# Relu fused into VectorE's add out of PSUM, y held unscaled, and a fourth-power range check on w1

## The chip, the cores and the metric

One core of one Trainium2 chip. The metric is the device time of one execution in microseconds (us), as the median of several runs. Each comparison was made on one chip, but not all on the same one. PE is TensorE's matmul, PEld its weight load, DVE VectorE, ACT ScalarE, POOL GpSimd, SP the engine whose queue issues most stores.

## The reference

```python
batch, m, k, h, n = 16, 512, 768, 3072, 768       # x, w1, b1, w2: standard normal, fp32
y = np.maximum(np.matmul(x, w1) + b1, 0)
return np.matmul(y, w2).astype(np.float32)
```

## The kernel before

Both products run in fp16 with a Strassen-like scheme of seven block products p1 to p7, whose sums are built partly in PSUM. So PE goes on accumulating into a bank *after* ACT has copied the intermediate sum out of it: p6 follows the copy of p1, p7 the copy of p6, in the same bank "a". The rows of x are done in 8 blocks, the hidden dimension in 2 halves, which gives 16 iterations (the first product of the first one is done plainly, so 15 x 6 = 90 groups have the code below); the product groups of neighbouring iterations are interleaved on PE.

```python
def first(self, it, t):                       # one group of the first product
    def copy(name, ps, bias):                 # ACT: intermediate sum out of PSUM
        nc.scalar.activation(out=g[name], in_=ps, func=ACTF.Identity, bias=bias, scale=YS)
    def add(slot, ps, s):                     # DVE: PSUM times 1/16 plus the copy
        nc.vector.scalar_tensor_tensor(out=y[:, slot], in0=ps, scalar=YS, in1=g[s],
                                       op0=ALU.mult, op1=ALU.add)
    ...
    def p3():
        mm(g["c"], self.XS4, self.B22, False)
        add(self.A12, g["c"], "s2")
        nc.vector.tensor_scalar(out=y[:, 0:3], in0=y[:, 0:3], scalar1=0.0,
                                scalar2=None, op0=ALU.max)          # the relu of three blocks
    def p4():
        mm(g["a"], self.XA22, self.T4, False)
        nc.scalar.activation(out=y[:, self.A21], in_=g["a"], func=ACTF.Relu, ...)
        self.sums_y(y)                        # DVE: four sums for the second product
```

fp16 can overflow, so the kernel gathers sums of squares of all inputs on ACT, tests them late, and falls back to a general path when they are out of bounds:

```python
def stat_w(self, stat, c, t, w):              # half c, tile t of w1 or w2
    ...
    self.nc.scalar.activation(out=junk, in_=flat[:, 0:4], func=ACTF.Square,
                              accum_out=self.stat[:, i:i + 1])
...
for t in range(TP):                           # when: iteration c*8+1 for w1, c*8+2 for w2
    at = (t // 2, 1 + 3 * (t % 2))            # (output group, block product)
    put("m2", c * NSB + 1, *at, self.stat_w, "w1", c, t, self.w1s)
    put("m2", c * NSB + 2, *at, self.stat_w, "w2", c, t, self.w2s)
```

## Time and profile before

| | before |
|---|---|
| time, median of 3 | 901.82 us |
| span in the profile | 899.9 us |
| PE, DVE, ACT busy | 98%, 67%, 45% |
| from the 71st matmul's start to the last one's | 877.7 us |

A hole below is the time between two matmul starts beyond the usual spacing (216 ns after one of 512 columns, 162 after one of 384). The lines of the page and how they are read are in the prediction.

### The profile page before, as it was taken

To read this page: it belongs to the slowest core of one execution; us is meant where nothing else is said; L and a number is where in the kernel's file an instruction comes from. 1 tells how busy PE (TensorE), PEld (TensorE's weight loads), DVE (VectorE), ACT (ScalarE), POOL (GpSimd) and SP (SyncE) were. 2 spreads that over 40 slices of the span, in tenths; PEclk is the share of its full clock that TensorE was granted. 3 is DMA by queue.
4 is the path that set the end of the run, shared out by engine and by line. 5 is a ranking of instruction groups with operands and counts; after the bars stand their busy time and mean duration, and the time that the engine had idled before them with its cause. 6 is when DMAs were issued, how large, how long until landed. Compare 5 with 4: busy or idle time off the path is not lost. (4 is left out here: it accounts for less than half of the span.)

```text
span 899.9 us, 13094 instructions
## 1 busy us (share of the span) xinstructions
PE 883.6 (98%) x4775; PEld 468.0 (52%) x4775; DVE 601.2 (67%) x1103; ACT 407.5 (45%) x698; POOL 84.0 (9%) x143
## 2 busy tenths in 40 slices
PE   7999999999999999999999999999999999999997
PEld 4455454554545555454554545545455554545544
DVE  2597838658475674837748677685776858667574
ACT  4757685765555546525434055262513315042220
POOL 7200000010000000012001000101001010010100
PEclk9999999999999999999999999999999999999999
DMA  9999999588675945576749434635445364350613
GB/s 203 201 238 191 339 172 284 106 245 172 148 247 110 307 93 194 210 154 136 193 164 388 161 121 179 210 138 176 151 183 176 129 199 184 120 176 36 211 53 125
DMA packets 106472, 162.53 MB, mean 181 GB/s; under 512 B 67852, under 2 KB 81956, under 8 KB 104356
## 3 DMA queue, kind: packets, MB, share of 16 engines
q1 hardware_dynamic: 67696, 114.44, 37.0%
q0 software_dynamic: 38384, 46.41, 26.0%
q8 instruction: 39, 0.64, 0.3%
q10 hardware_dynamic: 324, 0.80, 0.3%
q14 instruction: 29, 0.24, 0.1%
HBM read 95.37 MB, written 76.48 MB: 191 GB/s over the span
## 5 line engine op out<-in xcount | busy, mean ns | idle before, releaser
L440 PEld LDWEIGHTS <-y 128*128 128x128 f16 x2688 | 263.0, 98 | 190.3 <-issue 5.0
L359 PEld LDWEIGHTS <-w1s 128*128 128x128 f16 x1890 | 184.9, 98 | 212.8 <-issue 1.9
L440 PE MATMUL a<-w2s,y 128*128 128x384 f16 x1536 | 276.2, 326 | 4.2 <-DVE o L445 1.9
L359 PE MATMUL a<-x,w1s 128*128 128x512 f16 x1080 | 267.7, 379 | 0.9 <-DVE y L369 0.8
L365 ACT ACTIVATE s<-a,b1y 128x512 f32<-128x512 f32 x180 | 123.8, 688 | 313.2 <-PE a L359 310.7
L359 PE MATMUL c<-x,w1s 128*128 128x512 f16 x540 | 145.9, 379 | 0.1
L440 PE MATMUL c<-w2s,y 128*128 128x384 f16 x768 | 145.7, 326 | 0.0
L445 DVE SCALAR_TENSOR_TENSOR o<-a,s 128x384 f32<-128x384 f32 x64 | 35.6, 556 | 74.7 <-PE a L440 70.8
L315 DVE TENSOR_TENSOR y<-y 128x512 f16<-128x512 f16 x96 | 40.8, 425 | 65.5 <-ACT y L403 52.9
L369 DVE SCALAR_TENSOR_TENSOR y<-a,s 128x512 f16<-128x512 f32 x90 | 61.6, 685 | 30.6 <-ACT s L365 30.6
L403 ACT ACTIVATE y<-a,b1y 128x512 f16<-128x512 f32 x90 | 61.9, 687 | 30.1 <-PE a L359 30.1
L359 PE MATMUL b<-x,w1s 128*128 128x512 f16 x270 | 73.0, 379 | 0.0
L440 PE MATMUL b<-w2s,y 128*128 128x384 f16 x384 | 72.9, 326 | 0.0
L424 POOL DMA_DIRECT2D o<-out_dram x64 | 34.6, 546 | 388.4 <-DMA out_dram<-o 175.9
L317 DVE TENSOR_TENSOR y<-y 128x1024 f16<-128x1024 f16 x96 | 66.4, 692 | 3.3
L365 ACT ACTIVATE s<-c,b1y 128x512 f32<-128x512 f32 x90 | 61.9, 688 | 8.0 <-PE c L359 8.0
L454 ACT ACTIVATE s<-a 128x384 f32<-128x384 f32 x64 | 31.3, 488 | 71.7 <-PE a L440 71.7
L369 DVE SCALAR_TENSOR_TENSOR y<-b,s 128x512 f16<-128x512 f32 x90 | 61.6, 684 | 2.7 <-PE b L359 1.1
L369 DVE SCALAR_TENSOR_TENSOR y<-c,s 128x512 f16<-128x512 f32 x90 | 61.4, 682 | 0.4
L445 DVE SCALAR_TENSOR_TENSOR o<-b,s 128x384 f32<-128x384 f32 x64 | 35.6, 556 | 31.9 <-PE b L440 15.6
L398 DVE TENSOR_SCALAR y<-y 128x1536 f16<-128x1536 f16 x90 | 50.4, 560 | 3.1
L252 ACT ACTIVATE junk<-xn 128x768 f16<-128x768 f16 x60 | 50.5, 842 | 0.3
(67 smaller groups left out, 439.1 us busy)
## 6 DMA issues: line engine op xcount, KB each, us to landing
out_dram<-o SPq DMA_DIRECT2D x127, 384.0 KB, 3.6
o<-out_dram POOLq DMA_DIRECT2D x64, 384.0 KB, 4.1
xd<-x SPq DMA_DIRECT2D x8, 2688.0 KB, 12.0
x<-xd SPq DMA_DIRECT2D x8, 2688.0 KB, 9.7
xn<-in_x_dram POOLq DMA_DIRECT2D x15, 768.0 KB, 10.3
w1s<-in_w_dram POOLq DMA_DIRECT2D x24, 192.0 KB, 6.5
w2d<-w2t SPq DMA_DIRECT2D x6, 672.0 KB, 3.8
w2s<-w2d SPq DMA_DIRECT2D x6, 672.0 KB, 9.7
```

The costliest lines, as they stand in the source:

```text
L252: self.nc.scalar.activation(out=junk[:, 0:2].rearrange("p a n -> p (a n)"), in_=rows, func=ACTF.Square, accum_out=self.stat[:, i:i + 1])
L315: tt(out=y[:, self.S1], in0=y[:, self.A21], in1=y[:, self.A22], op=ALU.add)
L317: tt(out=y[:, self.S3:self.S2 + 1:self.S2 - self.S3], in0=y[:, self.A21:self.S1 + 1], in1=a11, op=ALU.subtract)
L359: nc.tensor.matmul(ps, lhsT=w[:, slot, k, :], rhs=x[:, xslot, k, :], start=(start and k == 0), stop=(k == 2), skip_group_check=True)
L365: nc.scalar.activation(out=g[name], in_=ps, func=ACTF.Identity, bias=bias, scale=YS)
L369: nc.vector.scalar_tensor_tensor(out=y[:, slot], in0=ps, scalar=YS, in1=g[s], op0=ALU.mult, op1=ALU.add)
L398: nc.vector.tensor_scalar(out=y[:, 0:3], in0=y[:, 0:3], scalar1=0.0, scalar2=None, op0=ALU.max)
L403: nc.scalar.activation(out=y[:, self.A21], in_=g["a"], func=ACTF.Relu, bias=bias1, scale=YS)
L424: self.nc.gpsimd.dma_start(out=o[:, half, :], in_=self.rows_of(it, j, half))
L440: nc.tensor.matmul(ps, lhsT=ys[t][:, op, j * P:(j + 1) * P], rhs=ws[t][:, slot, :], start=(start and t == 0), stop=(t == self.TP - 1), ski ...
L445: nc.vector.scalar_tensor_tensor(out=o, in0=ps, scalar=inv, in1=s, op0=ALU.mult, op1=ALU.add)
L454: nc.scalar.activation(out=to, in_=ps, func=ACTF.Copy, scale=inv)
```

## The change

Its intent is to relieve VectorE. An operation that adds two tensors and clamps the sum between two constants makes the separate relu needless. Both of its constants are bounds, so none is left for a scale, and y is no longer held as 1/16 of itself. An unscaled y comes nearer to fp16's limit, which asks for a sharper bound on w1, a sum of fourth powers, and ACT squares the tile twice.

```diff
-X_HI, W1_HI, W2_HI, B_HI = 64.0, 1500.0, 8000.0, 60000.0
+X_HI, W1_HI, W2_HI, B_HI = 34.0, 50.0, 8000.0, 1300.0
 ...
-        self.nc.scalar.activation(out=junk, in_=flat[:, 0:4], func=ACTF.Square,
+        src = flat[:, 0:4]
+        if stat == "w1":
+            self.nc.scalar.activation(out=junk, in_=src, func=ACTF.Square)
+            src = junk
+        self.nc.scalar.activation(out=junk, in_=src, func=ACTF.Square,
                                   accum_out=self.stat[:, i:i + 1])
 ...
-            nc.vector.scalar_tensor_tensor(out=y[:, slot], in0=ps, scalar=YS, in1=g[s],
-                                           op0=ALU.mult, op1=ALU.add)
+            nc.vector._custom_dve(TENSOR_ADD_SAT, out=y[:, slot], in0=ps, in1=g[s], s0=F_MAX,
+                                  s1=0.0)
 ...
-            nc.vector.tensor_scalar(out=y[:, 0:3], in0=y[:, 0:3], scalar1=0.0,
-                                    scalar2=None, op0=ALU.max)
 ...                                           # second product
-            nc.vector.scalar_tensor_tensor(out=o, in0=ps, scalar=inv, in1=s,
-                                           op0=ALU.mult, op1=ALU.add)
+            nc.vector.tensor_tensor(out=o, in0=ps, in1=s, op=ALU.add)
```

Cut: ACT's `scale=YS` and `scale=inv` and the scaling of b1 go, w1's lower bound becomes 2 instead of 8, and the bounds are filled in to the fourth power for w1.

More of the change, by code (lines that the diff above doesn't have):

```diff
@@ L6 @@
 from concourse._compat import with_exitstack
+from concourse.dve_ops import TENSOR_ADD_SAT
 from concourse.masks import make_identity
@@ L18 @@
 P = 128
-YS = 1.0 / 16.0
-X_HI, W1_HI, W2_HI, B_HI = 64.0, 1500.0, 8000.0, 60000.0
-X_LO, W1_LO, W2_LO = 1.0, 8.0, 0.5
+F_MAX = 3.0e38
+X_HI, W1_HI, W2_HI, B_HI = 34.0, 50.0, 8000.0, 1300.0
+X_LO, W1_LO, W2_LO = 1.0, 2.0, 0.5
 def general_path(ctx, tc, xf, w1, b1, w2, of):
@@ L158, in constants @@
         at = 0
-        for width, hi, lo in ((nw, W1_HI, W1_LO), (nw, W2_HI, W2_LO), (nx, X_HI, X_LO),
-                              (nb, B_HI, 0.0)):
-            nc.gpsimd.memset(self.high[:, at:at + width], hi * hi)
-            nc.gpsimd.memset(self.low[:, at:at + width], lo * lo)
+        for width, hi, lo in ((nw, W1_HI ** 4, W1_LO ** 4), (nw, W2_HI ** 2, W2_LO ** 2),
+                              (nx, X_HI ** 2, X_LO ** 2), (nb, B_HI ** 2, 0.0)):
+            nc.gpsimd.memset(self.high[:, at:at + width], hi)
+            nc.gpsimd.memset(self.low[:, at:at + width], lo)
             at += width
@@ L177, in turn_bias @@
         nc.tensor.transpose(ps[:, 0:nb], rows, self.ident[0:nb, 0:nb])
-        nc.vector.tensor_scalar(out=self.b1y, in0=ps[:, 0:nb], scalar1=YS, scalar2=None,
-                                op0=ALU.mult)
+        nc.vector.tensor_copy(out=self.b1y, in_=ps[:, 0:nb])
         nc.scalar.activation(out=self.stat[:, self.nstat - nb:], in_=ps[:, 0:nb],
@@ L333, in step @@
             nc.scalar.activation(out=y[:, slot], in_=ps, func=ACTF.Relu,
-                                 bias=self.bias_of(0, half, t), scale=YS)
+                                 bias=self.bias_of(0, half, t))
         m1, m2 = (self.XA11, self.XA12), (self.XA21, self.XA22)
@@ L364, in copy @@
             g[name] = self.s_tile(name)
-            nc.scalar.activation(out=g[name], in_=ps, func=ACTF.Identity, bias=bias,
-                                 scale=YS)
+            nc.scalar.activation(out=g[name], in_=ps, func=ACTF.Identity, bias=bias)
         def add(slot, ps, s):
-            nc.vector.scalar_tensor_tensor(out=y[:, slot], in0=ps, scalar=YS, in1=g[s],
-                                           op0=ALU.mult, op1=ALU.add)
+            nc.vector._custom_dve(TENSOR_ADD_SAT, out=y[:, slot], in0=ps, in1=g[s], s0=F_MAX,
+                                  s1=0.0)
         def p1():
@@ L403, in p4 @@
             nc.scalar.activation(out=y[:, self.A21], in_=g["a"], func=ACTF.Relu,
-                                 bias=bias1, scale=YS)
+                                 bias=bias1)
             self.sums_y(y)
@@ L435, in second @@
         g = {}
-        inv = 1.0 / YS
         def mm(ps, op, slot, start):
@@ L453, in take @@
             if part is None:
-                nc.scalar.activation(out=to, in_=ps, func=ACTF.Copy, scale=inv)
+                nc.scalar.activation(out=to, in_=ps, func=ACTF.Copy)
             else:
```

## The prediction

Passages that no trace of this case shows are cut from the text below, and the cuts are marked. Its sum came to 901.8 + 4.6 = 906.4 us. The one term that a cut touches is step 3's, where the estimated time of the plain add is gone; it enters the sum as 0. What the trace gives is the time of the scaled adds that are replaced, 685 ns (L369) and 556 ns (L445); that the new operations would take as long was the estimate. The eight banks of rival (b) are the program's own eight PSUM buffers (pools of 3, 2 and 3).

> **What bounds the kernel now.** I read the page first (busy shares and slices), then the groups by shape, then the waits of PE alone, then the order in time of two stretches. In section 1 PE is busy 98%, DVE 67%, ACT 45%; in section 2 PE is at 9 or more in all slices but the first and the last, and ACT is highest early.
>
> ```profile
> PE 883.6 (98%) x4775; PEld 468.0 (52%) x4775; DVE 601.2 (67%) x1103; ACT 407.5 (45%) x698; POOL 84.0 (9%) x143
> ...
> PE   7999999999999999999999999999999999999997
> ...
> ACT  4757685765555546525434055262513315042220
> ```
>
> A busy PE need not be a fast PE, so I checked its pace. In the timeline three 512-column matmuls start in 0.647 us (216 ns each) and six 384-column ones in 0.974 us (162 ns each), though the records read 379 and 326 ns. The program has 1890 + 144 of the first kind and 2688 of the second: 2034 x 0.216 + 2688 x 0.162 = about 876 us. Of the span of 899.9 us that leaves some 24: 9.7 before the first real matmul, about 5.5 after the last one (last add and store), 2 for transposes, and 6 to 7 of holes. The holes that the waits of PE put on DVE:
>
> ```profile
> PE a L440 <- DVE o L445: 1.9, 2, 1.7
> PE a L440 <- DVE w2s L219: 1.4, 1, 1.4
> PE a L440 <- DVE s L445: 0.9, 1, 0.9
> PE a L359 <- DVE y L369: 0.8, 1, 0.8
> ```
>
> They and two of 0.2 to 0.3 us in the start sum to 5.5 us. That is all that a faster VectorE could ever win. These are the groups that the change touches:
>
> ```profile
> L369 DVE SCALAR_TENSOR_TENSOR y<-a,s 128x512 f16<-128x512 f32 x90 | 61.6, 685 | 30.6 <-ACT s L365 30.6
> ...
> L398 DVE TENSOR_SCALAR y<-y 128x1536 f16<-128x1536 f16 x90 | 50.4, 560 | 3.1
> L315 DVE TENSOR_TENSOR y<-y 128x512 f16<-128x512 f16 x96 | 40.8, 425 | 65.5 <-ACT y L403 52.9 <-ACT y L333 12.4
> ...
> L227 ACT ACTIVATE junk<-w1s 128x1536 f16<-128x1536 f16 x12 | 17.8, 1482 | 0.2
> ```
>
> L398 is the separate relu (90 times); L315, which follows it on DVE, spends 52.9 us waiting for ACT's relu of the fourth product. L227 is the range statistic of w1, 12 times.
>
> [...]
>
> **The change part by part.** (1) **Gone: 90 relus** of 0.560 us, 50.4 us of DVE time, 601 to about 551. The order of instructions is otherwise unchanged on every engine but for part 4. What the relu's time is worth is read in the stretch of first products:
>
> ```profile
> 306.67 0.68 DVE L369 SCALAR_TENSOR_TENSOR y<-c,s 128x512 f16<-128x512 f32 x1
> ...
> 307.39 0.56 DVE L398 TENSOR_SCALAR y<-y 128x1536 f16<-128x1536 f16 x1
> 307.94 0.69 ACT L403 ACTIVATE y<-a,b1y 128x512 f16<-128x512 f32 x1
> ...
> 308.66 0.42 DVE L315 TENSOR_TENSOR y<-y 128x512 f16<-128x512 f16 x1 [0.71 <-ACT y L403]
> ```
>
> DVE finishes the relu at 307.95 and then idles 0.71 us until ACT's activation, which follows the last product on PE, is done. Without the relu the same L315 starts at the same time, after an idle time of some 1.2 us. Gain for PE: 0. The two holes in the final group (0.8 and 0.9 us, at 865 and 869) also lie behind an L315 that waited for L403 with DVE idle (0.53 and 0.42 us), so they stay. The 1.4 us hole at 47 us and the 1.7 us hole at 138 us have other DVE work in front. I allow 0.
>
> (2) **270 adds become add-and-clamp** of an estimated 0.685 us: 0. (3) 384 scaled adds in the second product become plain adds, 0.556 us [...]: 0. ACT's scale becomes 1: 0.
>
> (4) **Added: 12 squares on ACT**, since a fourth power needs two passes over w1. Each costs 1.48 us, and the second pass waits for the first's result on the same engine (some 0.04 us, the gap between dependent statistics in the trace): 1.52 us, 18 us of ACT time. Six of them stand near 550 us, where ACT idles 13.5 us right after the group: six times 1.52 is 9.1, hidden. The other six stand between 107 and 131 us, and there ACT has no room:
>
> ```profile
> 113.50:132.40 18.90, 18.90 (x118) 11.35 (x116) 6.25 (x9) 18.47 (x37) 2.10 (x3) 1.00 0.91 166
> ```
>
> In this stretch of 18.9 us (columns: length, then PE, PEld, DVE, ACT, POOL) ACT is busy 18.47. Five squares more, 7.6 us, can only be had by lagging, and PE needs ACT: it may go on accumulating into a bank only after ACT has copied the intermediate sum out of it.
>
> ```profile
> 121.66 1.48 ACT L227 ACTIVATE junk<-w1s 128x1536 f16<-128x1536 f16 x1
> ...
> 123.05 0.19 ACT L227 ACTIVATION_READ_ACCUMULATOR junk<-w1s 128x1 f32 x1
> 123.26 1.48 ACT L227 ACTIVATE junk<-w1s 128x1536 f16<-128x1536 f16 x1
> ...
> 125.58 2.11 PE L440 MATMUL a<-w2s,y 128*128 128x384 f16 x12
> ...
> 125.72 0.47 ACT L454 ACTIVATE s<-a 128x384 f32<-128x384 f32 x1
> ```
>
> Take the copy at 125.72, done at 126.19. It sits behind two statistics. PE's next product in that bank (the second half of the run at 125.58) starts at 126.56, 0.37 us later. Now add the lag. The first square (107.7) meets 1.3 us of ACT idle time and is absorbed.
> - Copy done at 118.02 moves by 2 x 1.52 to 121.06; PE wanted the bank at 119.73: PE loses 1.3.
> - Copy done at 126.19 moves by 4 x 1.52 to 132.3; PE, late by 1.3, wanted it at 127.9: loses 4.4 (5.7 in all).
> - Copy done at 131.78 moves by 5 x 1.52 to 139.4; PE wanted it at 138.8: loses 0.6 (6.3 in all).
>
> (5) **Given back:** just after, PE already loses 2.05 us in the kernel before (0.23 at 135.7 and 1.82 at 136.5), because a VectorE add waited for a store to free its output buffer:
>
> ```profile
> 134.49 0.56 DVE L445 SCALAR_TENSOR_TENSOR o<-b,s 128x384 f32<-128x384 f32 x1 [4.25 <-DMA out_dram<-o]
> ...
> 138.35 1.14 PE L440 MATMUL a<-w2s,y 128*128 128x384 f16 x6 [1.66 <-DVE o L445]
> ```
>
> That store follows a copy of ACT's that ends at 127.4; it moves by 6.1 to 133.5. In the kernel before the store was issued at about 128.6, behind another, and took 5.9 us; with 4.2 (median of this stretch) to 5.9 us it lands at 137.7 to 139.4. From that add to PE's restart it was 3.86 us, so PE restarts at 141.6 to 143.2. PE, late by 6.3, would want it at 136.3 + 6.3 = 142.6. So it restarts at 142.6 to 143.2, against 138.35 before: a net loss of 4.3 to 4.9 us. Sum: 901.8 + 4.6 = **906.4 us**.
>
> **Rivals.** (a) **VectorE's relief reaches PE**: for it, DVE is 86% busy in the first-product stretch (3.87 of 4.50 us) and some PE holes name it; against it, DVE idles in front of L315. At most 5.5 us, 896 us. (b) **ACT's squares are hidden**, by the eight banks or a lead of ACT that I misjudge: about 901.8 us. For it, ACT is 45% busy over the whole; against it, the stretch above. (c) **The add-and-clamp is slower than one add**, and DVE becomes the bound of the first-product stretch. With the relu gone DVE has about 0.56 + 0.5 = 1.1 us to spare in each group of 4.53 us, so three adds may each grow by 0.35 us, to 1.04. [...] Only the custom nature of the operation speaks for it. (d) The delay of ACT reaches later loads (it frees the buffers of x) and opens a second hole: 1 to 4 us more.
>
> **Range and chances.** The mechanism of part 4 gives 4 to 6.3 us; hidden or helped it falls to 901, with (d) it rises to 910. Range 902.5 to 909.5. Faster by over 2% needs 18 us, more than all holes together: 1%. Slower by over 2% needs (c): 5%. Within 2%: 94%.
>
> **What would show it.** In the profile after: DVE near 551 us, ACT near 425; the clamping adds at 0.68 us (over 1.04 refutes part 2); the first sum of y (L315 before) waiting for ACT's relu some 0.56 us longer in each group; PE's waits with a new line on ACT's copy, about 6 us, all between 119 and 140 us, and none near 550; the hole behind the store at 138 us smaller than 2 us. If PE's waits in that stretch do not grow, part 4 is wrong; if PE's old DVE holes shrink elsewhere, part 1 is.

## The result, and the profile after

The changed kernel takes 908.2 us (median of 4 runs, 906.39 to 908.34), the kernel before 901.38 in the same comparison. The ratio is 1.0073, with a 95% interval of 1.0056 to 1.0091. It is a small loss that is clear of the noise.

Section 1 of the page after, its first line:

```profile
PE 885.0 (98%) x4775; PEld 468.7 (52%) x4775; DVE 551.9 (61%) x1013; ACT 425.0 (47%) x710; POOL 83.5 (9%) x143
```

DVE lost 49.3 us of work and ACT gained 17.5; PE's work is the same 4775 matmuls. The groups by shape after (columns: line, engine, operation, operands and count; busy us, mean ns of one; idle time before, with its releasers):

```profile
L319 DVE TENSOR_TENSOR y<-y 128x512 f16<-128x512 f16 x96 | 40.8, 425 | 116.1 <-ACT y L405 103.7 <-ACT y L337 12.4
L373 DVE CUSTOM_DVE_ANT_0 y<-a,s 128x512 f16<-128x512 f32 x90 | 61.7, 685 | 32.2 <-ACT s L369 32.0
...
L231 ACT ACTIVATE junk<-junk 128x1536 f16<-128x1536 f16 x12 | 17.8, 1483 | 0.4
...
L229 ACT ACTIVATE junk<-w1s 128x1536 f16<-128x1536 f16 x12 | 17.8, 1482 | 0.3
```

The add-and-clamp takes 685 ns, as the scaled add did. The first sum of y, now L319, waits for ACT's relu 103.7 us instead of 52.9: 50.8 us more, 0.56 us a group. The 90 relus had taken 50.4 us: their time turned into waiting. The waits of PE after:

```profile
PE a L441 <- ACT s L454: 5.4, 2, 4.2
...
PE a L441 <- DVE w2s L219: 1.4, 1, 1.4
PE a L441 <- DVE s L446: 0.9, 1, 0.9
PE a L363 <- DVE y L373: 0.8, 1, 0.8
```

New is a wait for ACT's copies, twice. Gone from the list are the 1.9 us on DVE's add L445: 1.66 behind the store at 138 us and 0.24 at 193 us. The other three stand as before, although DVE has less to do. The timeline after, at the two new holes (start, duration, what; idle time before in brackets):

```profile
120.69 0.47 ACT L454 ACTIVATE s<-a 128x384 f32<-128x384 f32 x1
...
121.21 1.14 PE L441 MATMUL a<-w2s,y 128*128 128x384 f16 x6 [1.20 <-ACT s L454]
...
131.89 0.47 ACT L454 ACTIVATE s<-a 128x384 f32<-128x384 f32 x1
...
132.41 2.08 PE L441 MATMUL a<-w2s,y 128*128 128x384 f16 x6 [4.21 <-ACT s L454]
...
132.69 0.15 PEld L441 LDWEIGHTS <-y 128*128 128x128 f16 x1 [0.17 <-issue]
...
133.00 0.15 PEld L441 LDWEIGHTS <-y 128*128 128x128 f16 x1 [0.17 <-issue]
133.32 0.15 PEld L441 LDWEIGHTS <-y 128*128 128x128 f16 x1 [0.17 <-issue]
```

Both products start 0.05 us after a copy ends. After the second hole something was not foreseen: the six matmuls take 2.08 us instead of 1.14, and the weight loads come every 0.32 us, not every 0.16. The windows of the same trace (columns as in the prediction; after POOL come the granted PE clock, the DMA share and GB/s), the hole first and then the matmuls behind it:

```profile
128.30:132.41 4.11, 0.00 (x0) 0.00 (x0) 0.00 (x0) 4.05 (x7) 0.00 (x0) 0.90 0.24 96
132.41:135.63 3.22, 3.22 (x13) 1.61 (x12) 1.03 (x2) 3.22 (x8) 1.41 (x2) 0.59 0.36 23
```

ACT works through the whole hole. Then PE's granted clock is 0.59 on average over 3.2 us; the trace's clock record shows half speed for 3.41 us, from 131.62 to 135.03 us, of which the beginning fell into the hole.

### The profile page after: what moved, and what is told of

It is laid out like the page before. It is cut to its first block, busy times and chain, and to the rows that moved or that the text cites. A ratio compares the mean times of both kernels' runs of the same rounds, so it can differ in the third digit from the quotient of the medians.

```text
span 904.8 us, 13016 instructions
## 1 busy us (share of the span) xinstructions
PE 885.0 (98%) x4775; PEld 468.7 (52%) x4775; DVE 551.9 (61%) x1013; ACT 425.0 (47%) x710; POOL 83.5 (9%) x143
## 5 line engine op out<-in xcount | busy, mean ns | idle before, releaser
L369 ACT ACTIVATE s<-a,b1y 128x512 f32<-128x512 f32 x180 | 123.7, 687 | 305.4 <-PE a L363 302.3
L319 DVE TENSOR_TENSOR y<-y 128x512 f16<-128x512 f16 x96 | 40.8, 425 | 116.1 <-ACT y L405 103.7
L446 DVE TENSOR_TENSOR o<-a,s 128x384 f32<-128x384 f32 x64 | 35.6, 556 | 83.4 <-PE a L441 73.3
L373 DVE CUSTOM_DVE_ANT_0 y<-a,s 128x512 f16<-128x512 f32 x90 | 61.7, 685 | 32.2 <-ACT s L369 32.0
L369 ACT ACTIVATE s<-c,b1y 128x512 f32<-128x512 f32 x90 | 61.9, 688 | 8.1 <-PE c L363 8.1
L373 DVE CUSTOM_DVE_ANT_0 y<-b,s 128x512 f16<-128x512 f32 x90 | 61.6, 684 | 3.0 <-PE b L363 1.3
L373 DVE CUSTOM_DVE_ANT_0 y<-c,s 128x512 f16<-128x512 f32 x90 | 61.5, 683 | 0.4
L446 DVE TENSOR_TENSOR o<-b,s 128x384 f32<-128x384 f32 x64 | 35.6, 556 | 26.3 <-PE b L441 15.6
L446 DVE TENSOR_TENSOR s<-a,o 128x384 f32<-128x384 f32 x64 | 35.6, 556 | 19.5 <-PE a L441 19.5
## 6 DMA issues: line engine op xcount, KB each, us to landing
xn<-in_x_dram POOLq DMA_DIRECT2D x15, 768.0 KB, 10.6
```

The costliest lines, as they stand in the source:

```text
L319: tt(out=y[:, self.S1], in0=y[:, self.A21], in1=y[:, self.A22], op=ALU.add)
L373: nc.vector._custom_dve(TENSOR_ADD_SAT, out=y[:, slot], in0=ps, in1=g[s], s0=F_MAX, s1=0.0)
L446: nc.vector.tensor_tensor(out=o, in0=ps, in1=s, op=ALU.add)
```

## The experiments

All traces were also compared matmul by matmul with that of the kernel before. "Loss" below is the growth of the time from the 71st matmul's start to the last one's; it leaves out the head.

| run | what | median us | ratio to before, 95% interval | loss in the trace, us |
|---|---|---|---|---|
| after | the change | 908.2 | 1.0073 (1.0056 to 1.0091) | +4.8 |
| after_again | the change, second trace | 907.38 | 1.0057 (1.0038 to 1.0076) | +5.1 |
| a1 | a2 with wrong bounds: general path, void | 2912.43 | 3.2298 (3.2234 to 3.2363) | - |
| b1 | before + second squares | 907.35 | 1.006 (1.004 to 1.008) | +5.2 |
| a2 | after without second squares | 902.29 | 1.0003 (0.9988 to 1.0018) | -0.3 |
| c1 | before + second squares, late half only | 901.61 | 0.9995 (0.9975 to 1.0016) | -0.4 |
| g1 | before + two more squares in the early half | 914.26 | 1.013 (1.0108 to 1.0152) | +11.8 |
| e1 | after + dummy matmuls ahead of the hole | 906.93 | 1.0047 (1.0025 to 1.0068) | +4.4 |
| d1 | after, statistics spread | 899.6 and 899.83 | 0.9974 twice | -2.5 twice |
| d2 | before, statistics spread | 900.04 | 0.9976 (0.9962 to 0.999) | -2.5 |

### The second squares alone, and everything but them

b1 adds only the second pass to the kernel before (with bounds to match):

```diff
+        src = flat[:, 0:4]
+        if stat == "w1":
+            self.nc.scalar.activation(out=junk, in_=src, func=ACTF.Square)
+            src = junk
```

> The kernel before with only the second square for w1 added (with bounds to match); relu, scaled adds and scaled y as they were. Theory ScalarE: ratio 1.006 to 1.008 like the changed kernel, with the same PE waits of about 1.3 and 4.3 us behind copies near 120 and 128 us and one half-clock window after the second. Rival fused add: 1.000. Rival DVE load: if VectorE's 50 us more of relus matter in that stretch, more than 1.009.

The whole loss is there, at 1.006, with DVE as busy as ever (601.9 us). The first line of PE's waits in b1 that is not the load of x:

```profile
PE a L444 <- ACT s L458: 5.4, 2, 4.2
```

Its matmul starts show holes of 1.36 and 4.38 us, equal to those of the changed kernel to 0.01 us, and the same slow matmuls behind the second. DVE's 50 us of relus neither add to nor take from it.

a1 was the opposite, the changed kernel with one pass: I squared W1_HI = 50 for the bound, but the squares are summed over 1536 x 128 elements with a mean of at least 1, so the sum is near 200,000 or above, and the bound was 2500. The range check failed and the general path ran.

> The changed kernel with the w1 statistic back to one square per tile (second pass on ScalarE gone; the fused relu, the plain adds and unscaled y stay). Theory ScalarE (the 5 second passes between 113 and 137 us stop PE through the copies out of PSUM, and that is all that the change costs): back to the kernel before, ratio 1.000 (0.998 to 1.002), no PE wait on the copies near 120 and 128 us, no half-clock window there. Rival fused add (the add-and-clamp or the plain adds cost time that the traces hide): stays at 1.005 to 1.008. Rival relief (the fused relu helps PE): below 0.998.

It gave 2912.43 us, which tells nothing about the theory. a2 has the bounds of the kernel before:

```diff
-        for width, hi, lo in ((nw, W1_HI ** 4, W1_LO ** 4), ...
+        for width, hi, lo in ((nw, 1500.0 ** 2, 8.0 ** 2), ...
-        if stat == "w1":
-            self.nc.scalar.activation(out=junk, in_=src, func=ACTF.Square)
-            src = junk
```

> The run a1 again, mended: a1 kept bounds of w1 that do not fit one square, so that the range check failed and the general path ran (2912 us). Here the bounds are those of the kernel before; otherwise the changed kernel with one square per tile of w1. Theory ScalarE: ratio 1.000 (0.998 to 1.002), PE's holes those of the kernel before, of which the one near 138 us stays. Rival fused add: 1.005 to 1.008. Rival relief: under 0.998.

1.0003: the fused relu, 270 add-and-clamps, 384 plain adds and the unscaled y together are worth nothing measurable. The wait on ACT's copies is gone from PE's list, and the one behind the store is back:

```profile
PE a L438 <- DVE o L443: 1.9, 2, 1.4
```

### Only the place matters

c1 adds the second pass in the late half of w1 only, where ACT has room.

```diff
+        if stat == "w1" and c == 1:
+            self.nc.scalar.activation(out=junk, in_=src, func=ACTF.Square)
+            src = junk
```

> The kernel before with the second square only for the second half of w1, whose six statistics stand near 550 us where ScalarE then idles 13.5 us. Theory ScalarE (only the place matters): 9 us of work added, ratio 1.000 (0.998 to 1.002), ScalarE busy about 416 us. Rival (each square costs wherever it is): half of the loss, 1.003 to 1.004.

0.9995. The same window of the kernel before and of c1, in that order:

```profile
540.00:575.00 35.00, 35.00 (x204) 19.83 (x203) 24.04 (x44) 14.19 (x21) 2.13 (x4) 1.00 0.52 192
```

```profile
540.00:575.00 35.00, 35.00 (x204) 19.77 (x202) 23.96 (x44) 23.76 (x27) 2.13 (x4) 1.00 0.52 192
```

ACT goes from 14.19 to 23.76 us of 35, and PE is busy for all 35 in both. Over 9 us of extra work cost nothing here; in the full stretch 7.5 us cost 5. The two places differ in more than ACT's room: in the late half the second product adds its sums on DVE (`take`), and ACT's last copy for it ends at 467 us, so less on PE waits for ACT there. c1 doesn't separate the two; d1 below does, with the squares in the early half.

g1 doubles the dose in the early half (two more squares per tile; one in the late half).

```diff
+        if stat == "w1":
+            for _ in range(2 - c):
+                self.nc.scalar.activation(out=junk, in_=src, func=ACTF.Square)
+            src = junk
```

> The kernel before with two extra squares per tile for the first half of w1, one for the second. Theory ScalarE (a full stretch: each further square there goes straight to the end): lag at the three copies 7.0, 13.1 and 16.1 us, PE stopped about 5.3, 7.4 less the clock's share, 2 us, less some 2 us given back at the store: 12 to 13.5 us over the kernel before, ratio 1.013 to 1.015. Rival (a fixed cost, such as one lost window of clock): about 1.007 as with one extra square.

1.013, and PE's wait on the copies doubles:

```profile
PE a L445 <- ACT s L459: 10.6, 3, 5.6
```

Two of its holes, of 4.8 and 5.7 us, are each followed by a stretch of matmuls at half clock (mean granted clock of its profiled run 0.995, of the change's 0.997). I had expected PE to stop for 5.3, somewhat under 7.4 and 2 us at the three copies; it was 4.8, 5.7 and 0.6. The loss in the trace grows from 5.2 to 11.8 us, by 6.6, for five squares or 7.6 us more. Of this, 5.2 us are longer waits for the copies (10.6 against 5.4), and the second stretch at half clock is most of the rest. So in a stretch that full most of each square reaches the end. The measured times (914.26 against 907.35, not of the same rounds) grow by 6.9.

### The clock

e1 puts 14 matmuls that nobody reads (2.3 us) on PE ahead of the product that waits at 128 us in the changed kernel.

```diff
+    def warm(self):
+        ps = self.pb.tile([P, self.MH], FP32, name="b")
+        for _ in range(14):
+            self.nc.tensor.matmul(ps[:, 0:self.NH], lhsT=self.w1s[0][:, 0, 0, :],
+                                  rhs=self.w2s[0][:, 0, :], start=True, stop=True)
 ...
+        put("m2", 1, 3, 0, self.warm)
```

> The changed kernel with 14 dummy matmuls of 384 columns (2.3 us) on PE just ahead of the product that waits for ScalarE at 128 us; they write a PSUM buffer that nothing reads. Theory half-clock follows an idle time (the slow matmuls after the 4.4 us hole are the clock's answer to it): the hole shrinks to about 2.1 us, no window of half clock near 130 us, the slow matmuls of 320 ns gone, and the 1.2 us that they cost with them; then the third copy stops PE by up to 0.6 us, so 0.5 to 1 us faster than the changed kernel. Rival (the slow matmuls come from something else, weight loads or PSUM, at this point of the program): still slow, and the time unchanged or longer.

The windows of e1, the stretch with the dummies and the hole, then the matmuls behind it:

```profile
129.00:133.42 4.42, 2.48 (x17) 1.37 (x14) 0.00 (x0) 4.36 (x7) 0.00 (x0) 1.00 0.22 89
133.42:136.50 3.08, 3.08 (x19) 1.85 (x19) 1.52 (x2) 3.08 (x8) 1.41 (x2) 1.00 0.37 23
```

The hole shrank to 2.1 us, the clock stayed at 1.00, and the slow matmuls are gone. Now the third copy stops PE for 0.62 us. From the matmul ahead of the first hole to the last, e1 loses 4.4 us against 4.8 and 5.1 in the two traces of the changed kernel. The timed difference (1.0047 against 1.0057, not the same rounds) is within the intervals, so only the traces show this gain, 0.4 and 0.7 us where 0.5 to 1 was expected.

### Spread statistics

d1 is the changed kernel with the twelve early statistics put one pair to an iteration; d2 does the same to the kernel before.

```diff
             for t in range(TP):
                 at = (t // 2, 1 + 3 * (t % 2))
+                if c == 0:
+                    put("m2", 1 + t, 0, 1, self.stat_w, "w1", c, t, self.w1s)
+                    put("m2", 1 + t, 3, 1, self.stat_w, "w2", c, t, self.w2s)
+                    continue
```

> The changed kernel, with the twelve statistics of the first halves of w1 and w2 spread, one pair each over six iterations (w1 in the first output group, w2 in the last), so that ScalarE never lags; all second passes stay. Theory ScalarE: no PE wait on its copies, no half-clock window; also the old hole at 138 us (a store that follows a late ScalarE copy) goes: ratio 0.996 to 1.000. Rival (the second passes cost wherever they are): 1.003 or more.

> The kernel before (separate relu, one square for w1) with the statistics spread as in d1_spread. Theory (VectorE's relief is worth nothing at PE even with ScalarE's lag gone, and d1's gain is the hole at 138 us): the same as d1_spread, ratio of d2 to d1 0.999 to 1.001, PE's holes the same to 0.1 us. Rival relief (the fusion helps once ScalarE is out of the way): d2 slower than d1 by 0.002 or more.

> d1_spread again, on the same chip as d2: 899.6 us, ratio to the kernel before 0.996 to 0.999, to d2 0.999 to 1.001.

d1 takes 899.6 us, ratio 0.9974 (0.9954 to 0.9993), and again 899.83, ratio 0.9974 (0.996 to 0.9989): it beats both kernels, with all second squares in it. The window that was full in the kernel before, in d1:

```profile
113.50:132.40 18.90, 18.90 (x119) 11.38 (x117) 6.99 (x12) 12.88 (x29) 2.15 (x3) 1.00 0.99 189
```

ACT is at 12.88 us of 18.90, not 18.47. The first waits of PE in d1 after the load of x, with nothing on ACT or a store any more:

```profile
PE a L441 <- DVE w2s L219: 1.4, 1, 1.4
PE a L441 <- DVE s L446: 0.9, 1, 0.9
PE a L363 <- DVE y L373: 0.8, 1, 0.8
```

So the hole at 138 us of the kernel before was ACT's lag too: ACT's late copy held the store, and the store held the output buffer. It makes 2.05 of the 2.5 us; the other 0.4 are a smaller hole of the kernel before at 193 us, also behind an L445, which d1 and d2 don't have either. d2 has the same holes and the same loss of -2.5 us, and on one chip the two take 899.83 and 900.04 us. The separate relu and the wait after it in d2:

```profile
L398 DVE TENSOR_SCALAR y<-y 128x1536 f16<-128x1536 f16 x90 | 50.7, 563 | 3.1
L315 DVE TENSOR_TENSOR y<-y 128x512 f16<-128x512 f16 x96 | 40.8, 425 | 65.1 <-ACT y L403 52.6 <-ACT y L333 12.4
```

The relu still lies in front of a wait for ACT. Even with ACT's lag out of the way the fusion is worth nothing to the time.

### The second trace of the change

> The changed kernel again, for a second trace: its first had a span of 904.8 us, three others 906.6 to 906.8. Theory half-clock: the difference is how long PE runs at half clock after its 4.4 us hole or when the window falls. Rival store: it is the hole near 138 us behind the store (0 in the first trace, up to 2 us). Whichever it is, this trace shows the holes of 1.4 and 4.4 us at about 120 and 128 us again.

The second trace (span 905.8 us) has holes of 1.36 and 4.38 us again, the half clock once and for 3.41 us again, and no hole behind the store near 138 us. The half clock begins a little later against the hole, so that one matmul more is slow (eight spacings of 0.32 us between weight loads, not seven); with this the second trace loses 5.1 us, the first 4.8. So neither of the two reasons that I had offered accounts for 2 us between runs. The head (16.4 to 17.6 us up to the 71st matmul; in it the wait for the first rows of x, 5.0 to 5.8) makes up to 1.2 us. The rest of the spread, 906.4 to 908.3 us for the change and 899.3 to 905.4 for the kernel before, stays open. The runs of d1 and d2 spread by 1 us only (899.4 to 900.4), which for the kernel before suggests its hole behind the store, but no trace of such a run shows it.

## Why the prediction was right

The predicted 906.4 us, 902.5 to 909.5, held 908.2, and "within 2%" was right. By its own steps:

- **Relu gone, no gain for PE (step 1): right.** The sum of y waits 0.56 us longer in each of 90 groups; a2 (1.0003) and d1 against d2 show no gain with and without ACT's lag.
- **Add-and-clamp and plain adds at the old durations (steps 2 and 3): right.** 685 and 556 ns, against 685 and 556 for the scaled adds before.
- **Late squares hidden, early ones not (step 4): right.** c1 shows the first, b1 the whole of the second. The first two copies stopped PE for 1.36 and 4.38 us, against the predicted 1.3 and 4.4. The dependent square started 1.51 us after the one before it (1.52). The 0.04 us in that figure was no gap between dependent statistics, though: in the trace before it lies between the read of an accumulator and the next, independent statistic (116.02 to 116.06). That 0.03 was measured is luck.
- **The third copy, 0.6 us: not in the changed kernel.** The half clock, which the sum has no term for, had made PE 1.2 us later by itself (seven matmuls at 0.32 us instead of 0.16 and one in part), so that the copy was ready. e1, with the clock kept up, shows the 0.62 us. A hole of 4.4 us stood in my own sum, and I did not ask what it would do to the clock. The traces show this much: the holes of 4.4 us (the change) and of 4.8 and 5.7 us (g1) were followed by half clock, those of 1.4 us (the change) and 2.1 us (e1, 1.00 in both windows) not. In the first trace of the change the clock fell to half at 131.62 us, 3.6 us after its hole began, and came back at 135.03; of these 3.41 us 0.8 were still idle, so PE had worked for 2.6 us by then. The stretches of that clock record up to the kernel's end last 122.880, 3.413 and 767.999 us, or 36, 1 and 225 times 3.413 us; the trace of the kernel before has one of 890.879 us, 261 times as long. Where between 2.1 and 4.4 us of idle time the clock begins to fall, and whether the idle time alone decides it, these runs do not show.
- **Given back at the store (step 5): right, a little larger.** Of the 2.05 us nothing was left in either trace. At the product that resumed at 138.35 us, the shift between the traces, without that of the head, is 5.07 - 0.12 = 4.95 us, against 4.3 to 4.9.
- **Rivals:** relief (a) fell by a2 and d2, hiding (b) by b1, a slow operation (c) by its 685 ns; a later second hole (d) is in no trace.

The trace's 4.8 to 5.1 us match the 4.6 of the sum, but that they match so well is in part luck: the third copy's 0.6 us didn't come, the half clock's 1.2 weren't in the sum, and the store gave back 2.05 us instead of 1.4 to 2.0. The medians differ by 6.8 us, and the second comparison by 5.85; that excess is the spread left open above.

## What to carry to other kernels

An engine that is busy 45% of the whole can be full for 19 us: look at the busy time in the very stretch where work is added, and at who waits for the work that stands behind it on that engine (here PE for a copy, with ACT busy for 4.05 of the hole's 4.11 us), before taking its idle share as room. Work saved on an engine is worth nothing where the next instruction waits for another engine anyway. Statistics and other work with no deadline belong spread out, or where the engine idles; here moving them was worth more than the fusion.
